# Seven products instead of eight: the second half's output projection of a hybrid decoder layer by Strassen's scheme

## The chip, the cores and the metric

The kernel runs on one NeuronCore of one Trainium2 chip. Its time is the device time in microseconds (us) of one execution; shown is the median of several. The engines are TensorE (PE, with its weight loads as PEld), VectorE (DVE), ScalarE (ACT), GpSimd (POOL) and SyncE (SP), which here issues every DMA. Each engine works through its own instructions in order and waits on semaphores for the others.

## The reference

One layer over 1024 tokens of 1024 channels in float32. A mixer, made of a recurrence over 8 heads (RWKV-7) and a causal convolution of width 31, each giving 512 channels, is followed by an output projection, and that by a gated feed-forward part with a short convolution; each is normed before and after and added to its input. What the change touches is one line:

```python
x = x + _rms_norm(mix, norm_post_mix)       # mix = concatenate([rwkv_out, c]) @ w_out
#   rwkv_out: 1024 tokens x 512      c: 1024 tokens x 512      w_out: 1024 x 1024
h = _rms_norm(x, norm_pre_ffn)              # and from here the feed-forward part
```

For one half of the tokens (512) this product is 512 x 1024 by 1024 x 1024. Cut into two by two blocks, the activations are A11 (first 256 tokens, recurrent channels), A12 (first 256 tokens, convolution channels), A21 and A22 (the last 256 tokens); the weight has blocks B11 to B22 of 512 x 512.

## The kernel before, in words

The tokens are handled in two halves of 512 and, in the mixer, in quarters of 256; a quarter has four chunks of 64, which the recurrence takes one after the other. Every matrix product is done with operands split into a rounded high part and a low remainder (`split`: ACT casts the high part, then POOL or DVE subtracts it from the source), and three matmuls per pair of tiles: high x high, high x low, low x high. A weight tile of 256 KB is brought by `weight`: an SP DMA into one of the raw buffers (tag `wr`, three in pool `wp`, and two more in pool `wq` that only the feed-forward part uses), an ACT cast, and a subtraction by POOL, or by DVE where `low_pool` is false.

`mixer` writes the work as streams with priorities (`PRIO`); a scheduler puts each engine's instructions in an order worked out from priorities and from estimated times. The recurrence and what prepares it come first (`rwkv`), then the norm of the first half for the feed-forward part (`top`), norms, convolution, and last projections (`proj`), which fill TensorE where the others wait. `prepare(q)` runs the four recurrence chunks of quarter q-1 between the steps that prepare quarter q; `finish` norms and gates a quarter's result into `mixr`, a tile of 512 channels x 512 tokens. `conv` and `conv_norm` give the four `co` tiles. While the last quarter's recurrence runs (`prepare(4)`), the first nine blocks of the first half's feed-forward part (`EARLY`, `ffn_pair`, 48 matmuls each) fill TensorE.

Then `w_out(1, ...)` projects the second half. All eight activation tiles are split into four `l8` buffers, the split waiting for `W[3].merged`. For each of four groups of 256 output columns and each of eight row tiles of the weight, two tiles of rows to a load, there are four token tiles and three matmuls of 256 columns. `evac` multiplies a finished bank by the post-norm's weight (`post_mix`), squares it on ACT with a sum per token into `ssq`, and stores the product to `mixd` in DRAM. The load of the second column group's first weight is the mark `self.start`: loads of the feed-forward stage are issued behind it, so that the first gate matmuls (`gates`) can run between the groups. `norm_ffn(1, ...)` reads `ssq` and `mixd` back.

The feed-forward part already has a product of this kind: `ffn_down` by seven products, with its weight sums made on POOL by `four_sums` in `weight_sums`.

Of the kernel before, what the change touches and what calls it, by code (L numbers as in the profile page):

```python
# [22 lines left out]
P = 128  # L23
# [3 lines left out]
HALF = 512  # L27
QUARTER = 256
# [8 lines left out]
CONV_W = 31  # L37
# [10 lines left out]


BUFS = {"v": 2, "gd": 1, "pt": 6, "kk": 1, "l8": 5, "ca": 6, "ck": 6, "r": 2,  # L50
        "mixr": 1, "co": 4, "po": 1, "c": 4, "t2": 2}

EARLY = 9

JOINT = 13
PLAIN = FT - JOINT

RAW, MORE_RAW, PAIRS, MORE_PAIRS = 3, 2, 2, 1

PRIO = {"first": -1000, "top": 100000, "rwkv": 1000, "norm": 200000, "conv": 300000, "proj": 400000}  # L60


PARAMS = [
# [37 lines left out]
class Trunk:  # L101
# [62 lines left out]
    def split(self, hi, lo, src, pool=False):  # L164

        eng = self.nc.gpsimd if pool else self.nc.vector
        return self.nc.scalar.copy(hi, src), eng.tensor_tensor(lo, src, hi.bitcast(F32), ALU.subtract)  # L167

    def wtile(self, tag, shape, dt=F32):

        pool = next(self.homes[tag]) or self.wp
        bufs = {self.wp: (RAW, PAIRS), self.wq: (MORE_RAW, MORE_PAIRS)}[pool][tag != "wr"]
# [28 lines left out]
    def setup(self):  # L201
        nc, tc, ctx, a = self.nc, self.tc, self.ctx, self.a
        pool = lambda name, **kw: ctx.enter_context(tc.tile_pool(name=name, bufs=1, **kw))
        self.cp = pool("const")
        self.small = ctx.enter_context(tc.tile_pool(name="small", bufs=4))
        self.wp = ctx.enter_context(tc.tile_pool(name="wp", bufs=1))
        self.wq = ctx.enter_context(tc.tile_pool(name="wq", bufs=1))
        self.hp = ctx.enter_context(tc.tile_pool(name="hp", bufs=2 * KT))
        self.dp = pool("dram", space=DRAM)
        self.rowp = pool("rowp")  # L210
        self.psum = pool("psum", space=PSUM)
        cp = self.cp
# [12 lines left out]
        self.lows = self.dp.tile([22, 2, P, 4, P], F32, name="lows")  # L225
        self.sums = self.dp.tile([4, HT, P, 512], F32, name="sums")
        self.plain = self.dp.tile([PLAIN, P, HALF], F32, name="plain")
        self.usums = self.dp.tile([4, P, 512], F32, name="usums")
        self.ecarry = cp.tile([P, 2, 12, 2], F32, name="ecarry")

# [65 lines left out]
    def pair(self, what, pool):  # L296
        return tuple(pool.tile([P, HALF], F32R, tag="h", name=self.nm(what)) for _ in range(2))
# [534 lines left out]
        return mark  # L832


    def setup_ffn(self, ctx):
# [23 lines left out]
    def norm_ffn(self, h, row, piece, hs, ahead=2, tags=("pn",), dg=None, pool=None):  # L859


        nc = self.nc
        rows, diags = [], []
        cut = lambda c: slice(c * 512, (c + 1) * 512)

        def channels(tp):
            if not tp:
                hs.extend(self.pairs("f", pool))
            ts = slice(2 * tp, 2 * tp + 2)
            self.channels(rows[ts], "pre_ffn", hs, slice(tp * 256, (tp + 1) * 256), tags, diags[ts] or None)  # L870
# [3 lines left out]
        nc.vector.tensor_reduce(r[:, 0:4], self.ssq[:, 4 * h:4 * h + 4], AX.X, ALU.add)  # L874
        self.rstd(r[:, 4:8], r[:, 0:4], 1.0 / D, RMS_EPS)
        for t in range(4):
            if t == ahead:
                channels(0)
            tt = 4 * h + t
            rs = slice(tt * P, (tt + 1) * P)  # L880
            x, s = row(), sf[:, t]
            nc.sync.dma_start(x, self.a["x"][rs])
            for c in range(2):
                m = piece()
                nc.sync.dma_start(m, self.mixd[rs, cut(c)])
                nc.vector.scalar_tensor_tensor(x[:, cut(c)], m, r[:, 4 + t:5 + t], x[:, cut(c)], ALU.mult, ALU.add)
                nc.scalar.activation(m, x[:, cut(c)], AF.Square, accum_out=s[:, c:c + 1])
            nc.sync.dma_start(self.x1d[rs], x)
            nc.vector.tensor_tensor(s[:, 2:3], s[:, 0:1], s[:, 1:2], ALU.add)
            self.rstd(s[:, 3:4], s[:, 2:3], 1.0 / D, RMS_EPS)  # L890
            if dg is None:
                nc.scalar.activation(x, x, AF.Copy, scale=s[:, 3:4])
            else:
                nc.vector.tensor_scalar(dg[:, t], self.con("ident"), s[:, 3:4], None, ALU.mult)
                diags.append(dg[:, t])
            rows.append((x[:, :512], x[:, 512:]))
            yield
        if ahead == 4:
            channels(0)
            yield  # L900
        channels(1)
# [363 lines left out]
    def mixer(self, sts):  # L1265
        nc, tc = self.nc, self.tc
        W = [None] * 4
        mixes = [None] * 2

        def project(h, hs, names):  # L1270
            with self.stream("proj"):
                for n in names.split():
                    if n == "w":
                        self.wa_in(h, hs, sts[h])
                    elif n == "g":
                        self.gate_in(h, hs, sts[h])
# [74 lines left out]
        with self.stream("norm"):  # L1351
            two = [self.tl("l8", [P, 2, D]) for _ in range(2)]
# [3 lines left out]
            hs = self.pairs("h")  # L1356
# [21 lines left out]
        hs = self.pairs("h")  # L1378
# [25 lines left out]
        conv_norm(1)  # L1404
        with self.stream("proj"):
            piece = lambda: self.tl("pt", [P, HALF])
            for i in range(EARLY):
                if i % 2 == 0:
                    two = self.row("row", 4)
                nc.sync.dma_start(self.early[i], self.ffn_pair(0, h0, i, piece, two[:, i % 2 * HALF:(i % 2 + 1) * HALF]))  # L1410
# [77 lines left out]
```

## Time and profile before

| | |
|---|---|
| three runs | 1251.70, 1251.86, 1258.57 us |
| median | 1251.86 us |
| profiled execution | 1257.58 us, span 1255.8 us |
| granted TensorE clock in it | 0.985 |
| TensorE busy | 1210.4 us (96%) |
| DVE, ACT, POOL busy | 72%, 58%, 40% |
| second half's output projection | 640.34 to about 698.3 us of the span |

A row of the windows view is one stretch: its ends and length, then for PE, PEld, DVE, ACT and POOL the busy time with the number of instructions, then the granted clock, the share of the DMA engines, and GB/s. A row of the timeline is start, duration, engine, line, operation, written tile <- read tiles, and in brackets the idle time before it with what ended it. The chain of waits gives start, duration and the instruction group on the path that ended last. A row of a tile or line view gives the shortest, median and longest duration, the first and last start. L140 is the matmul helper, L155 the transpose helper, L167 `split`, L184 the weight's DMA.

### The profile page before, as it was taken

What the parts mean: (1) busy time and instruction counts of PE and PEld (TensorE: products, weight loads), DVE (VectorE), ACT (ScalarE), POOL (GpSimd) and SP (SyncE); (2) the same over time, 40 slices, a digit from 0 to 9 for tenths busy, and PEclk for the clock granted to TensorE, in tenths of its full rate; (3) what the DMA queues carried; (4) which work ended last, traced back from release to release, by engine and by line L of the source; (5) the groups of instructions that cost most, each with busy time, mean ns of one, the idle gap of its engine ahead of it and who ended that gap; (6) DMA issues with size and microseconds to landing.
All of it is one profiled execution on the core that took longest, in us unless ns stands there. A gap on an engine that the chain in (4) does not pass through costs nothing.

```text
span 1255.8 us, 22979 instructions
## 1 busy us (share of the span) xinstructions
PE 1210.4 (96%) x8424; PEld 988.9 (79%) x8424; DVE 899.8 (72%) x1558; ACT 729.1 (58%) x1515; POOL 507.1 (40%) x447
## 2 busy tenths in 40 slices
PE   5999999999999998999999999999999999999997
PEld 4767777787778876778889888888888888888885
DVE  5285998898669989998640555666656679479667
ACT  7563564565955676466762576876555566554451
POOL 4343330001103331344563399998888850000002
PEclk9999998999999989999999999999999999999999
DMA  7644442333343353222364798894322335336413
GB/s 243 177 131 137 129 135 64 97 128 119 114 128 91 97 178 110 75 80 85 104 186 118 271 323 293 298 315 153 82 74 81 101 134 166 95 117 219 134 52 134
DMA packets 102912, 180.97 MB, mean 144 GB/s; under 512 B 14896, under 2 KB 21424, under 8 KB 102800
## 3 DMA queue, kind: packets, MB, share of 16 engines
q1 hardware_dynamic: 102800, 179.51, 45.6%
q8 instruction: 66, 1.08, 0.4%
q14 instruction: 46, 0.38, 0.1%
HBM read 138.44 MB, written 41.03 MB: 143 GB/s over the span
## 4 chain that ended last, share of the span: by engine, by line
PE 62%; DVE 6%; ACT 2%; issue 1%; DMA 1%; POOL 1%; POOLq 0%; DVEq 0%; ACTq 0%
PE pb L140 27%; PE xs L140 16%; PE pe L140 14%; PE Y L140 2%; PE pc L140 2%; DVE pc L431 2%; DMA pt<-mixd 1%; PE pc L155 1%; PE pe L155 0%; DVE x L1120 0%; DVE m L167 0%; DVE sub L606 0%; DVE nrow L1136 0%; DVE dw L608 0%; DVE t L797 0%
## 5 line engine op out<-in xcount | busy, mean ns | idle before, releaser
L167 POOL TENSOR_TENSOR wl<-wr,wh 128x512 fp32r<-128x512 f32 (+1 forms) x175 | 230.0, 1316 | 219.4 <-ACT wh L167 191.3
L140 PE MATMUL pb<-h,wh 128*128 128x512 f32 (+3 forms) x720 | 230.1, 399 | 2.5 <-ACT wh L167 1.0
L167 ACT CAST wh<-wr 128x512 fp32r<-128x512 f32 (+1 forms) x214 | 131.4, 615 | 131.8 <-issue 42.3
L140 PE MATMUL pb<-f,wh 128*128 128x512 f32 x648 | 205.0, 397 | 2.7 <-ACT wh L167 1.7
L431 DVE SCALAR_TENSOR_TENSOR pc<-c,params,pc 128x512 f32<-128x512 f32 x232 | 174.2, 751 | 8.7 <-ACT pc L428 4.7
L140 PEld LDWEIGHTS pb<-h,wh 128*128 128x128 f32 (+2 forms) x720 | 132.1, 189 | 35.4 <-ACT wh L167 2.7
L140 PE MATMUL pb<-h,wl 128*128 128x512 f32 (+3 forms) x360 | 146.8, 408 | 2.3 <-POOL wl L167 2.1
L140 PEld LDWEIGHTS pb<-f,wh 128*128 128x128 f32 x648 | 121.8, 190 | 28.8 <-ACT wh L167 2.1
L140 PE MATMUL pb<-f,wl 128*128 128x512 f32 x324 | 129.2, 399 | 0.9 <-POOL wl L167 0.9
L162 POOL TENSOR_TENSOR ss<-var,mhalf 128x1 f32<-128x1 f32 x16 | 11.4, 716 | 223.8 <-DVE var L161 223.0
L1076 POOL TENSOR_TENSOR b<-b,b 128x512 f32<-128x512 f32 x72 | 93.3, 1298 | 1.9 <-DMA wr<-ffn_up 0.5
L140 PEld LDWEIGHTS pb<-h,wl 128*128 128x128 f32 (+2 forms) x360 | 67.8, 188 | 20.5 <-POOL wl L167 4.0
L140 PE MATMUL xs<-f,wh 128*128 128x512 f32 x240 | 74.2, 390 | 0.4 <-DVE act L973 0.4
L167 POOL TENSOR_TENSOR wl<-b,wh 128x512 fp32r<-128x512 f32 x48 | 66.6, 1388 | 16.9 <-ACT wh L167 14.9
L140 PEld LDWEIGHTS pb<-f,wl 128*128 128x128 f32 x324 | 61.7, 190 | 14.8 <-POOL wl L167 1.7
L167 ACT CAST wh<-b 128x512 fp32r<-128x512 f32 x48 | 29.7, 618 | 60.0 <-PE pb L140 20.5
L140 PE MATMUL pe<-f,wh 128*128 128x512 f32 x208 | 64.1, 389 | 0.0
L721 POOL TENSOR_TENSOR XG<-r,GE 64x256 f32<-64x256 f32 x30 | 20.5, 683 | 89.3 <-DVE r L740 84.5
L140 PEld LDWEIGHTS xs<-f,wh 128*128 128x128 f32 x240 | 44.9, 188 | 10.0 <-DVE act L973 0.8
L192 ACT CAST wh<-wr 128x512 fp32r<-128x512 f32 (+2 forms) x44 | 26.5, 604 | 44.4 <-PE pb L140 31.2
L167 ACT CAST a<-act 128x512 fp32r<-128x512 f32 x50 | 30.0, 620 | 33.6 <-PE Y L140 19.1
L167 ACT CAST w<-wr 128x512 fp32r<-128x512 f32 x38 | 23.4, 622 | 40.7 <-PE Y L140 20.0
(419 smaller groups left out, 2952.3 us busy)
## 6 DMA issues: line engine op xcount, KB each, us to landing
wr<-ffn_up SPq DMA_DIRECT2D x99, 256.0 KB, 3.2
wr<-w_in SPq DMA_DIRECT2D x80, 256.0 KB, 2.9
b<-ffn_up SPq DMA_DIRECT2D x52, 256.0 KB, 2.7
b<-ffn_down SPq DMA_DIRECT2D x44, 256.0 KB, 4.5
sums<-b SPq DMA_DIRECT2D x44, 256.0 KB, 4.2
wr<-sums SPq DMA_DIRECT2D x44, 256.0 KB, 2.8
lows<-wl SPq DMA_DIRECT2D x40, 256.0 KB, 3.3
wl<-lows SPq DMA_DIRECT2D x40, 256.0 KB, 2.7
```

The lines of the kernel that those rows point to most:

```text
L140: return self.nc.tensor.matmul(out, lhsT, rhs, start=start, stop=stop, skip_group_check=skip)
L155: self.nc.tensor.transpose(out, in_, self.con("ident")[:n, :n])
L162: self.nc.gpsimd.tensor_tensor(out, v[:, :n], self.mhalf[:, :n], ALU.pow)
L167: return self.nc.scalar.copy(hi, src), eng.tensor_tensor(lo, src, hi.bitcast(F32), ALU.subtract)
L192: self.nc.scalar.copy(hi, raw)
L431: nc.vector.scalar_tensor_tensor(out, c[:, j:j + HALF], w(j), acc, ALU.mult, ALU.add)
L721: nc.gpsimd.tensor_tensor(x[64:128], R[64:128, gs], w.GE[64:128, c, gs].unsqueeze(2).broadcast_to([64, 4, CH]), ALU.mult)
L1076: sub = lambda o, x, y, op=ALU.subtract: self.nc.gpsimd.tensor_tensor(o, x, y, op)
```

## The change

The second half's projection becomes seven products of 256 x 512 by 512 x 512 (`w_out_shared`). Each has four row tiles of the weight, two token tiles and three matmuls of 512 columns. The sums of weight blocks (four for each row tile) are made by POOL with `four_sums` while the mixer runs, in a stream of the lowest priority behind project(1)'s `u0`, and stored in DRAM (`wsums`). The sums of activations are made by DVE in place or in freed `v` buffers, and the sums of products by DVE from PSUM. The first product, A11 x B11, is written ahead of the last early feed-forward block, its result copied to SBUF by ACT. In products 3 to 7 the low parts of the weights come by turns from DVE and POOL. The mark for the feed-forward loads is the 21st weight load. Pool `wq` is opened in the feed-forward stage only, which makes room for four `ws` buffers in the mixer.

```diff
-        "mixr": 1, "co": 4, "po": 1, "c": 4, "t2": 2}
+        "mixr": 1, "co": 4, "po": 1, "c": 4, "t2": 2, "ws": 4}
+START = 20
+LAST = 1
-PRIO = {..., "proj": 400000}
+PRIO = {..., "proj": 400000, "sums": 500000}
...
-        self.wq = ctx.enter_context(tc.tile_pool(name="wq", bufs=1))     # in setup
+        self.wq = pool("wq")                                             # in setup_ffn
+        self.wsums = self.dp.tile([4, 4, P, 512], F32, name="wsums")
...
+    def w_out_tile(self, k, c):
+        return self.a["w_out"][2 * c:2 * c + 2, k // 2, :, k % 2].rearrange("e p n -> p e n")
+    def w_out_sums(self):
+        for k in range(4):
+            b = [self.tl("ws", [P, 512]) for _ in range(4)]
+            for n in range(4):
+                nc.sync.dma_start(two(b[n]), self.w_out_tile(4 * (n // 2) + k, n % 2))
+            self.four_sums(*b, b[3])
+            for n, t in ((3, 3), (1, 1), (2, 0), (4, 2)):
+                nc.sync.dma_start(self.wsums[n - 1, k], b[t])
+    def w_out_shared(self, mixr, co, between):
...
+        A11 = split(a11)
...
+        def product(banks, src, acts, start, stop, turn=(False, True)):
+            hi, lo = acts
+            for k in range(4):
+                self.low_pool = turn[k % 2]
+                wh, wl = self.weight(src(k), [P, 2, 256], (self.mix, "ca", "ck"))
+                self.low_pool = True
+                self.marks.append(self.load)
...
+                for t in range(2):
+                    ts = slice(t * P, (t + 1) * P)
+                    self.mm(banks[t], hi[:, k, ts], wh, start=start and k == 0, stop=False, skip=True)
+                    self.mm(banks[t], hi[:, k, ts], wl, start=False, stop=False, skip=True)
+                    self.mm(banks[t], lo[:, k, ts], wh, start=False, stop=stop and k == 3, skip=True)
+        def out(src, q, c):
+            with self.tc.high_priority():
+                for t in range(2):
+                    o = self.tl("c", [P, CONV_W - 1 + HALF])[:, :512]
...
+                    nc.vector.tensor_tensor(o, src[t], post[c], ALU.mult)
+                    nc.scalar.activation(src[t], src[t], AF.Square, accum_out=self.ssq[:, tile_, c:c + 1])
+                    nc.sync.dma_start(self.mixd[tile_ * P:(tile_ + 1) * P, c * 512:(c + 1) * 512], o)
...
+        product(first, B(0, 0), A11, True, True, (True, True))
...
+                nc.scalar.copy(u[t], first[t])
+        between()
+        A12 = split(a12)
+        s3 = spare()
+        tt(s3, a11, a21, ALU.subtract)
+        each(a21, lambda k: a21[:, k], lambda k: a22[k], ALU.add)
+        s2 = spare()
+        tt(s2, a21, a11, ALU.subtract)
+        S2 = split(s2)
+        S1 = split(a21)
+        y = [self.bank("pe") for _ in range(2)]
+        product(y, B(1, 0), A12, True, True, (True, True))
+        add(y, u, y)
+        out(y, 0, 0)
+        x = self.xs
+        product(x, T(2), S2, True, True)
+        S3 = split(s3)
+        add(u, u, x)
+        y = [self.bank("pe") for _ in range(2)]
+        product(y, T(1), S1, True, True)
+        w = [self.tl("ws", [P, 512]) for _ in range(2)]
+        each(s2, lambda k: a12[k], lambda k: s2[:, k], ALU.subtract)
+        S4 = split(s2)
+        add(w, u, y)
+        z = [self.bank() for _ in range(2)]
+        product(z, T(3), S3, True, True)
+        A22 = split(a22)
+        add(x, w, z)
+        out(x, 1, 1)
+        product(y, B(1, 1), S4, False, True)
+        add(y, u, y)
+        out(y, 0, 1)
+        product(z, T(4), A22, False, True)
+        add(z, u, z)
+        out(z, 1, 0)
+        return self.marks[START]
...
-        project(1, hs, "u0 u1 u2 u3")
+        project(1, hs, "u0")
+        with self.stream("sums"), tc.issue_after(self.load.ins):
+            self.w_out_sums()
+        project(1, hs, "u1 u2 u3")
...
-            for i in range(EARLY):
+            for i in range(EARLY - LAST):
+                block(i)
         prepare(4)
         with self.stream("proj"):
-            self.start = self.w_out(1, mixes[1], [sts[1]["co", i] for i in range(4)], W[3].merged)
+            self.start = self.w_out_shared(mixes[1], [sts[1]["co", i] for i in range(4)],
+                                           lambda: [block(i) for i in range(EARLY - LAST, EARLY)])
```

More of the change, by code (lines that the diff above doesn't have):

```diff
@@ L56 @@
 PLAIN = FT - JOINT
+START = 20
+LAST = 1
 RAW, MORE_RAW, PAIRS, MORE_PAIRS = 3, 2, 2, 1
-PRIO = {"first": -1000, "top": 100000, "rwkv": 1000, "norm": 200000, "conv": 300000, "proj": 400000}
+PRIO = {"first": -1000, "top": 100000, "rwkv": 1000, "norm": 200000, "conv": 300000, "proj": 400000, "sums": 500000}
 PARAMS = [
@@ L171, in wtile @@
         pool = next(self.homes[tag]) or self.wp
-        bufs = {self.wp: (RAW, PAIRS), self.wq: (MORE_RAW, MORE_PAIRS)}[pool][tag != "wr"]
+        bufs = ((RAW, PAIRS) if pool is self.wp else (MORE_RAW, MORE_PAIRS))[tag != "wr"]
         return pool.tile(shape, dt, tag=tag, bufs=bufs, name=self.nm(tag))
@@ L832, in w_out @@
         return mark
+    def w_out_tile(self, k, c):
+        return self.a["w_out"][2 * c:2 * c + 2, k // 2, :, k % 2].rearrange("e p n -> p e n")
+    def w_out_sums(self):
+        nc = self.nc
+        two = lambda t: t.rearrange("p (e n) -> p e n", e=2)
+        for k in range(4):
[5 more added lines that the diff above has]
+                nc.sync.dma_start(self.wsums[n - 1, k], b[t])
@@ new lines, in w_out_shared, with pair, split, spare @@
+    def w_out_shared(self, mixr, co, between):
+        nc = self.nc
+        early, later = slice(0, QUARTER), slice(QUARTER, HALF)
+        f = lambda t: t.bitcast(F32)
+        tt = nc.vector.tensor_tensor
+        def pair():
+            t = self.tl("l8", [P, 2, 4, QUARTER], F32R)
+            return t[:, 0], t[:, 1]
+        def split(src):
+            hi, lo = pair()
+            if isinstance(src, list):
+                for k in range(4):
+                    self.split(hi[:, k], lo[:, k], src[k])
+            else:
+                self.split(hi, lo, src)
+            return hi, lo
+        def spare():
+            return self.tl("v", [P, 2, HALF]).rearrange("p l (b t) -> p (l b) t", b=2)
+        def each(out, x, y, op):
+            for k in range(4):
+                tt(out[:, k], x(k), y(k), op)
+        a11, a21 = mixr[:, :, early], mixr[:, :, later]
+        a12, a22 = ([t[:, ts] for t in co] for ts in (early, later))
+        A11 = split(a11)
+        post = [self.tl("c", [P, CONV_W - 1 + HALF])[:, :512] for _ in range(2)]
+        for c in range(2):
+            nc.sync.dma_start(post[c], self.a["post_mix"][:, c * 512:(c + 1) * 512].broadcast_to([P, 512]))
+        def product(banks, src, acts, start, stop, turn=(False, True)):
+            hi, lo = acts
+            for k in range(4):
+                self.low_pool = turn[k % 2]
+                wh, wl = self.weight(src(k), [P, 2, 256], (self.mix, "ca", "ck"))
+                self.low_pool = True
+                self.marks.append(self.load)
+                wh, wl = (w.rearrange("p e n -> p (e n)") for w in (wh, wl))
+                for t in range(2):
[7 more added lines that the diff above has]
+                    o = self.tl("c", [P, CONV_W - 1 + HALF])[:, :512]
+                    tile_ = 4 + 2 * q + t
+                    nc.vector.tensor_tensor(o, src[t], post[c], ALU.mult)
+                    nc.scalar.activation(src[t], src[t], AF.Square, accum_out=self.ssq[:, tile_, c:c + 1])
+                    nc.sync.dma_start(self.mixd[tile_ * P:(tile_ + 1) * P, c * 512:(c + 1) * 512], o)
+        def add(outs, xs, ys):
+            with self.tc.high_priority():
+                for o, x, y in zip(outs, xs, ys):
+                    tt(o, x, y, ALU.add)
+        B = lambda r, c: lambda k: self.w_out_tile(4 * r + k, c)
+        T = lambda n: lambda k: self.wsums[n - 1, k].rearrange("p (e n) -> p e n", e=2)
+        self.marks = []
+        first = [self.bank() for _ in range(2)]
+        product(first, B(0, 0), A11, True, True, (True, True))
+        u = [self.tl("ws", [P, 512]) for _ in range(2)]
+        with self.tc.high_priority():
+            for t in range(2):
+                nc.scalar.copy(u[t], first[t])
[34 more added lines that the diff above has]
+        return self.marks[START]
@@ L873, in norm_ffn @@
         sf = self.small.tile([P, 4, 4], F32, tag="sf", bufs=1, name=self.nm("sf"))
-        nc.vector.tensor_reduce(r[:, 0:4], self.ssq[:, 4 * h:4 * h + 4], AX.X, ALU.add)
+        nc.vector.tensor_reduce(r[:, 0:4], self.ssq[:, 4 * h:4 * h + 4, :2 if h else 4], AX.X, ALU.add)
         self.rstd(r[:, 4:8], r[:, 0:4], 1.0 / D, RMS_EPS)
@@ L1406, in mixer, with block @@
             piece = lambda: self.tl("pt", [P, HALF])
-            for i in range(EARLY):
+            def block(i):
                 if i % 2 == 0:
-                    two = self.row("row", 4)
-                nc.sync.dma_start(self.early[i], self.ffn_pair(0, h0, i, piece, two[:, i % 2 * HALF:(i % 2 + 1) * HALF]))
+                    two[:] = [self.row("row", 4)]
+                nc.sync.dma_start(self.early[i], self.ffn_pair(0, h0, i, piece, two[0][:, i % 2 * HALF:(i % 2 + 1) * HALF]))
+            two = []
+            for i in range(EARLY - LAST):
+                block(i)
         prepare(4)
         with self.stream("proj"):
-            self.start = self.w_out(1, mixes[1], [sts[1]["co", i] for i in range(4)], W[3].merged)
+            self.start = self.w_out_shared(mixes[1], [sts[1]["co", i] for i in range(4)],
+                                           lambda: [block(i) for i in range(EARLY - LAST, EARLY)])
         return h0
```

## The prediction

> **What bounds the kernel now.** I read the page first, then the busy time by stretches, then TensorE's own order of time around the second half's output projection.
>
> ```profile
> span 1255.8 us, 22979 instructions
> PE 1210.4 (96%) x8424; PEld 988.9 (79%) x8424; DVE 899.8 (72%) x1558; ACT 729.1 (58%) x1515; POOL 507.1 (40%) x447
> 320.00:360.00 40.00, 37.59 (x288) 29.33 (x287) 26.16 (x55) 31.19 (x69) 5.82 (x7) 1.00 0.35 106
> 360.00:400.00 40.00, 37.57 (x215) 30.30 (x214) 35.68 (x71) 21.10 (x40) 6.12 (x7) 0.96 0.32 100
> 520.00:600.00 80.00, 79.91 (x737) 63.82 (x729) 72.13 (x110) 48.00 (x105) 35.59 (x30) 1.00 0.29 85
> 624.00:640.00 16.00, 13.38 (x53) 10.03 (x52) 13.04 (x17) 13.64 (x27) 8.77 (x6) 0.91 0.36 114
> 640.00:698.00 58.00, 57.64 (x435) 55.42 (x434) 7.62 (x11) 19.27 (x51) 25.99 (x20) 1.00 0.51 146
> 700.00:900.00 200.00, 199.62 (x897) 164.99 (x896) 124.13 (x194) 140.04 (x296) 172.85 (x139) 1.00 0.78 263
> ```
>
> The columns after the stretch and its length are PE, PEld, DVE, ACT and POOL busy, granted clock, DMA share, GB/s. TensorE is the bound: 79.91 of 80 us, 57.64 of 58, 199.62 of 200. Holes are in the mixer (2.4 us in each of 320 to 360 and 360 to 400) and between 624 and 640 (2.6 us, at clock 0.91). So the change is worth what it takes off TensorE's work, plus holes closed, less holes opened. TensorE's timeline of the place:
>
> ```profile
> 632.64 0.39 PE L140 MATMUL pb<-f,wl 128*128 128x512 f32 x1
> 634.74 0.73 PE L140 MATMUL pb<-f,wh 128*128 128x512 f32 x2 [1.70 <-ACT wh L167]
> 636.39 0.50 PE L140 MATMUL pb<-f,wl 128*128 128x512 f32 x1 [0.92 <-POOL wl L167]
> ...
> 639.91 0.62 PE L140 MATMUL pb<-f,wl 128*128 128x512 f32 x1
> 640.34 11.71 PE L140 MATMUL pb<-wm,l 128*128 128x256 f32 x96
> ```
>
> Up to 639.91 this is the ninth early feed-forward block; at 640.34 the output projection begins. From 633.03 (end of the first row) to 640.34 only 12 matmuls run: x2 and x1 at the two waits, and three more such threes. The chain of waits then gives the paces:
>
> ```profile
> 652.05 11.52 PE xs L140 x96
> 666.33 5.47 PE xs L140 x24
> 683.31 5.47 PE pe L140 x24
> 688.78 8.76 PE pb L140 x73
> 698.28 2.13 DMA mixd<-t
> ```
>
> A matmul of 256 columns takes 11.52/96 = 0.120 us of the chain, one of 512 columns 5.47/24 = 0.228 us. The two groups of 24 are feed-forward gate blocks that already fill in behind the projection.
>
> **The change part by part. Matmuls.** Removed: 4 column groups x 8 row tiles x 4 token tiles x 3 (high and low parts) = 384 matmuls of 256 columns, 384 x 0.120 = 46.1 us. Check: 640.34 to 698.28 is 57.9, less 2 x 5.47 of filler 47.0. Added: 7 products x 4 x 2 x 3 = 168 matmuls of 512 columns, 168 x 0.228 = 38.3 us. TensorE saves **7.8 us**, all of it on the path, since TensorE is full. [...]
>
> **The hole at 633.** ACT's timeline shows what TensorE waited for:
>
> ```profile
> 628.78 1.28 ACT L452 ACT_TABLE_LOAD   x1
> 630.08 1.51 ACT L452 ACTIVATE co<-pc,params 128x128 f32<-128x128 f32 x4
> 631.46 0.63 ACT L167 CAST wm<-wr 128x512 fp32r<-128x512 f32 x1
> 631.97 2.19 ACT L167 CAST l<-co 128x512 fp32r<-128x512 f32 x4
> 634.05 0.63 ACT L167 CAST wh<-wr 128x512 fp32r<-128x512 f32 x1
> ```
>
> The ninth block's cast stood behind the convolution's last norm and the activation casts, which only the projection needs. The 7.31 us held 12 x 0.228 = 2.7 us of work, so the hole with its slow clock cost 4.6 us. After the change the first product (5.5 us; it needs only the early-token quarter of `mixr`) stands ahead of this block, and A12, S2 and S1 are needed only after the block. The last `co` lands at 631.6; the sum S1 (four of 0.42 us), S2 (1.25) and its split (ACT about 1.2, DVE 1.25) end near 637. The ninth block begins near 640.34 - 4.6 - 48 x 0.228 = 624.8 now; with the first product ahead of it, both are done at 624.8 + 5.5 + 10.9 = 641.2, and S2 is asked for only a product later, at 646.7. That is 9 us of cover, so I take the hole as closed: **4.6 us**. If the casts again queue ahead of the block's, nothing of it is won. (The 0.42 and 1.25 are these rows; they are 256 and 1024 elements wide.)
>
> ```profile
> L774 DVE TENSOR_TENSOR mixr<-mixr,pt 128x256 f32<-128x256 f32 x16 | 6.6, 420 | 5.7 <-ACT mixr L770 5.7
> L564 DVE TENSOR_TENSOR l<-l,gd 128x1024 f32<-128x1024 f32 x8 | 10.0, 1255 | 9.9 <-PE pe L140 9.9
> ```
>
> **Feeding the products.** Before, a weight load of 256 KB served 24 matmuls of 256 columns, 2.9 us; now it serves 6 of 512, 1.37 us. The raw buffers stay three.
>
> ```profile
> wr<-w_out SPq DMA_DIRECT2D x32, 256.0 KB, 2.8
> L167 ACT CAST wm<-wr 128x512 fp32r<-128x512 f32 x16 | 9.9, 621 | 11.5 <-PE xs L140 5.7 <-PE pb L140 3.6 <-DMA wr<-w_out 1.5
> L167 POOL TENSOR_TENSOR wm<-wr,wm 128x512 fp32r<-128x512 f32 x13 | 16.8, 1291 | 9.4 <-ACT wm L167 9.3
> L167 DVE TENSOR_TENSOR wl<-wr,wh 128x512 fp32r<-128x512 f32 x39 | 26.7, 685 | 0.6 <-ACT wh L167 0.6
> ```
>
> A buffer's turn is 2.8 (landing) + 0.62 (cast) + 0.99 (mean of POOL's 1.29 and DVE's 0.69, which alternate in products 3 to 7) = 4.4 us; over three buffers 1.47 us a weight against 1.37. Behind the first product stand 24 weights: 35.3 us of feeding against 32.8 of matmuls. The lower bound is 0 (six pair buffers, filled under the ninth block). The upper: DVE and POOL hold each other up. The same split of `co` took DVE 1118 ns a piece beside POOL and 680 without:
>
> ```profile
> L167 DVE TENSOR_TENSOR l<-co,l 128x512 fp32r<-128x512 f32 x4 | 4.2, 1118 | 1.1 <-ACT l L167 1.1
> L167 DVE TENSOR_TENSOR m<-co,m 128x512 fp32r<-128x512 f32 x4 | 2.6, 680 | 0.0
> 598.65 1.28 POOL L167 TENSOR_TENSOR wl<-wr,wh 128x512 fp32r<-128x512 f32 x1 [0.86 <-ACT wh L167]
> 598.74 1.74 DVE L932 TENSOR_TENSOR row<-pt,pt 128x512 f32<-128x512 f32 x1
> 567.86 0.68 DVE L932 TENSOR_TENSOR row<-pt,pt 128x512 f32<-128x512 f32 x1
> ```
>
> The DVE multiplication L932 took 1.74 instead of 0.68 us, to just after POOL's end at 599.93 plus its own time. In products 3 to 7 POOL's ten lows (12.9), DVE's ten lows (6.9), the splits of S3 and S4, the four differences and A22's four lows (about 6) make 25.8 us that must not overlap, in 27.3 us of matmuls. With a further 1 us of such waiting in each buffer's turn a weight takes 1.8 us: 43.2, that is 10.4 us lost. I take **2.5 us**, nearer the rows without waiting, as DVE is busy only 7.6 of 58 us there now. [...]
>
> **Sums of the product's vectors.** 14 additions from PSUM and 8 multiplications of 0.69 us on DVE, 8 squares and 2 copies on ACT (about 0.6): the only ones that could hold TensorE are those that free a bank, and each bank is asked for again a product (5.5 us) later, against some 3.5 us of work. Cost 0; if DVE's queue is late, this is part of the 10.4 above. After the last product gate matmuls follow in other banks, as now at 698. They are let in from the 21st load on, so holes of products 2 to 5 stay unfilled.
>
> **Weight sums in the mixer.** 16 POOL operations, 16 loads, 16 stores.
>
> ```profile
> L1076 POOL TENSOR_TENSOR b<-b,b x72: 1279/1295/1352, 724.5 to 1010.5; 128x512 f32<-128x512 f32 x72
> 383.32 1.27 POOL L167 TENSOR_TENSOR wl<-wr,wh 128x512 fp32r<-128x512 f32 x1 [3.14 <-DMA wr<-w_out]
> 382.04 0.18 DVE L608 TENSOR_TENSOR dw<-dw,sub 128x26 f32<-128x26 f32 x1
> 383.58 1.06 DVE L606 TENSOR_TENSOR sub<-dw 128x36 f32<-128x36 f32 x1
> L193 SPq DMA_DIRECT2D wl<-lows x23: 319/320/524, 283.8 to 377.3; - x23
> ```
>
> The last row places them: 23 of the second half's 44 loads of stored low parts (k, w, r, then u0 as the 19th to 22nd) come from 283.8 on, so the sums stand from about 284 to 340.
>
> 16 x 1.295 = 20.7 us of POOL, which has 5.8 of 40 us busy in 320 to 360, so POOL has room. But each can hold DVE as at 383.58: 1.06 instead of about 0.18, 0.88 us. Sixteen such are 14.1 us of DVE time; none is the lower end. DVE is idle 13.8 of 40 us there, and TensorE has the early blocks as cover from 520 on, so I take **1 us**. On SP's queue the stores wait for POOL, and project(1)'s loads stand behind them: at worst 4 sets x (5.2 us of sums, less 2.7 us for the weight ahead) = 10 us, at best nothing. I take 0, because in 700 to 900 the same pattern of stores runs with TensorE at 199.62 of 200. Moving the second weight pool (`wq`) into the feed-forward stage costs 0: its place was the mixer's constants, which are read for the last time ahead of the output projection, and the gate loads come after its 21st load.
>
> **Sum.** 7.8 + 4.6 - 2.5 - 1 = 8.9 us. The profiled execution took 1257.6 us (span 1255.8); it becomes 1248.7. The runs shown are 1251.70, 1251.86 and 1258.57, so the profiled one is like the longest. Applied to the median 1251.86: **1243 us**. One per cent, 12.5 us, is about what a measurement of this kernel can tell from no change.
>
> **The rivals.** *Everything flows.* Nothing lost in feeding or in the mixer: 12.4 us, 1239.4, a little less if a mixer hole closes too. For it: DVE nearly idle at 640 to 698. Against: 1.47 us a weight. Chance 0.18.
>
> *Feeding becomes the bound.* The upper price of 10.4 replaces 2.5: 8.9 - 7.9 = 1.0 us, 1251. For it: 25.8 of 27.3 us on DVE and POOL together, one in-order DVE queue that also carries the bank sums, and no filler before the 21st load. Against: six pair buffers ahead. Chance 0.20.
>
> *The sums in the mixer hold DVE.* Place: 284 to 340, where POOL would run 16 operations beside the chain of the recurrence. Price: 14.1 us, of which each that reaches TensorE opens a hole. It decides from 9.9 us on (12.4 less 2.5); at 14.1 the kernel is slower by 4.2: 1256. Against: TensorE has projections to do there. Chance 0.12.
>
> *The hole stays* (the scheduler's order leaves the casts ahead, so the moved block does nothing): 8.9 - 4.6 = 4.3 us, 1247.6. Inside the range; I count it with the forecast, whose band of 1239.5 to 1249 has 0.50.
>
> **How the numbers follow.** Range 1235 to 1257: from some 4 us under the full gain (mixer holes) to just over the slower rival. Faster by over 1% (under 1239.3): half of "everything flows" and the forecast's lower edge, with the execution-to-execution spread of 7 us, 0.21. Slower by over 1% (over 1264.4): the slower rival together with bound feeding, 0.07. Within 1%: 0.72.
>
> **What would show it.** Matmuls of `wm` 168 of 512 columns, 38 us together; no wait of over 1 us on L167 between the eighth early block and the second product; in products 2 to 7 TensorE's waits on ACT, POOL or DVE lows together near 2.5 us; the POOL sums somewhere from 284 to 340, and TensorE's busy time from 280 to 520 within 1 us of now. A granted clock under 1.0 during the products, or DVE operations of two SBUF inputs at 1.1 us and more all along them, would mean the feeding rival. The prediction is wrong if the reordering by the scheduler moves other mixer work by more than these terms.

## The result, and the profile after

The changed kernel takes **1273.35 us** (median of 6 runs, 1270.94 to 1276.24) against 1253.79 (1251.7 to 1258.57) for the kernel before beside it: ratio 1.0155, 95% interval 1.0133 to 1.0177. It is 1.55% slower. 1243 was forecast, in a range of 1235 to 1257, with 0.07 for slower by over 1%.

The page after, span and busy time (the profiled execution took 1276.24 us):

```profile
span 1274.5 us, 22686 instructions
PE 1210.9 (95%) x8208; PEld 980.4 (77%) x8208; DVE 931.5 (73%) x1595; ACT 737.5 (58%) x1518; POOL 530.0 (42%) x465
```

TensorE has 216 matmuls fewer and is busy just as long as before (1210.4). A busy time is not work: here it grew where the clock was low (14 `pe` matmuls took 1.16 us at 473.62, at clock 1.00 from 473.6 to 474.8, and 2.04 us at 482.43, at 0.50 from 482.4 to 484.5; the granted clock is 0.57 from 480 to 500). The span is 18.7 us longer. Where that arises is read best from a fixed mark. The store of the first early feed-forward block (tile `early`, first and last start) stands behind most of the mixer's work (the last quarter's recurrence still runs) and ahead of everything that the products touch. Before, then after (the code has more lines now: L1541 was L1410, `split` is L171, the matmul helper L144, the transpose helper L159, the weight's load L188, the load of stored low parts L197):

```profile
L1410 SPq DMA_DIRECT2D early<-row x9: 326/327/327, 521.7 to 644.0; - x9
```

```profile
L1541 SPq DMA_DIRECT2D early<-row x9: 320/327/441, 536.3 to 681.2; - x9
```

**14.6 us are lost before that mark**, and from it to the end of the span 738.2 us pass instead of 734.1, **4.1 more where 9.9 less were forecast**. (The two traces are of long executions: 3.8 us over the median before, 2.9 after.) The loss ahead of the mark shows at two places. The windows of before, then of after:

```profile
280.00:340.00 60.00, 59.04 (x454) 46.20 (x451) 48.98 (x88) 40.99 (x87) 11.82 (x16) 1.00 0.41 124
280.00:520.00 240.00, 226.84 (x2387) 186.96 (x2386) 204.86 (x398) 150.18 (x328) 59.03 (x64) 0.97 0.38 116
460.00:480.00 20.00, 18.17 (x230) 13.07 (x228) 13.96 (x34) 10.29 (x31) 4.78 (x6) 0.84 0.64 209
480.00:500.00 20.00, 16.91 (x175) 13.22 (x173) 19.28 (x50) 16.52 (x40) 3.61 (x6) 1.00 0.20 70
```

```profile
280.00:340.00 60.00, 55.94 (x393) 43.38 (x392) 48.07 (x80) 38.12 (x78) 33.03 (x32) 1.00 0.73 238
280.00:520.00 240.00, 220.19 (x2061) 181.73 (x2060) 194.59 (x378) 141.83 (x313) 75.28 (x75) 0.94 0.46 143
460.00:480.00 20.00, 13.01 (x163) 9.16 (x162) 13.63 (x28) 12.34 (x34) 4.52 (x6) 0.83 0.66 206
480.00:500.00 20.00, 18.67 (x152) 15.81 (x152) 11.36 (x31) 7.03 (x19) 2.70 (x5) 0.57 0.32 115
```

From 280 to 340, where the sums run, TensorE loses 3.1 us of work and the DMA share rises from 0.41 to 0.73. From 460 to 480, long after the last sum, it loses 5.2 us, and from 480 to 500 it runs at clock 0.57. Its timeline there:

```profile
477.29 0.41 PE L159 MATMUL xs<-const,v 128*64 128x128 f32 x2 [1.33 <-DVE r L744]
480.61 0.70 PE L144 MATMUL pe<-l,l 64*128 64x128 f32 x2 [2.92 <-DVE ca L560]
482.43 2.04 PE L144 MATMUL pe<-l,l 64*128 64x128 f32 x14 [0.72 <-DVE ca L560]
```

The `pe` bank that is asked for at 477.7 has yet to be read by DVE (`ca`, L560, in `scores` of the last quarter), which first does steps of a norm and of `finish` and comes to it at 479.71. Behind that matmul in TensorE's queue stands the recurrence chunk of the quarter before (L744 is the chunk's own step), so the chunk waits too, and no projection's matmul stands in the timeline from 473 to 500 to fill in.

In the products, the chain of waits leaves TensorE. It runs through two loads of `w_out` (2.80 us at 651.61 and 2.73 at 656.44), then through DVE:

```profile
663.79 1.96 DVE l L171 x2
665.74 0.60 issue
666.34 0.77 DVE v L880 x3
667.76 2.23 DVE l L171
669.99 0.60 DVE wm L171
670.59 0.66 DVE pt L1047
671.25 0.60 DVE pe L915
...
678.75 0.60 DVE wm L171
...
698.50 5.44 PE xs L144 x24
```

Splits of activation sums (`l`), a sum (`v`), the low part of a weight (`wm`), a tap of the moved ninth block (L1047), an addition of products (L915): one queue, one after another. GpSimd's holds are among them: the split of 1024 columns at 667.68 took 2.31 us beside a low part on GpSimd, the one at 665.20 took 1.21 without. From 660 to 680 DVE is busy 19.22 of 20 us and TensorE 13.89, at clock 0.88. The last row gives the pace of a 512-column matmul where nothing is late, 5.44/24 = 0.227 us.

### The profile page after: what moved, and what is told of

The parts are those of the page before. It is cut to its first block, busy times and chain, and to the rows that moved or that the text cites. A ratio compares the mean times of both kernels' runs of the same rounds, so it can differ in the third digit from the quotient of the medians.

```text
span 1274.5 us, 22686 instructions
## 1 busy us (share of the span) xinstructions
PE 1210.9 (95%) x8208; PEld 980.4 (77%) x8208; DVE 931.5 (73%) x1595; ACT 737.5 (58%) x1518; POOL 530.0 (42%) x465
## 4 chain that ended last, share of the span: by engine, by line
PE 73%; DVE 14%; ACT 5%; issue 3%; DMA 2%; POOL 2%; SPq 0%; POOLq 0%; DVEq 0%; ACTq 0%
PE pb L144 36%; PE xs L144 17%; PE pe L144 16%; DVE pc L435 4%; PE Y L144 2%; PE pc L144 2%; POOL wl L171 1%; PE pe L159 1%; DVE l L171 1%; DVE pt L504 1%; PE pc L159 1%; DVE dw L612 1%; DVE h L298 1%; DVE pt L1047 1%; DMA pt<-mixd 1%
## 5 line engine op out<-in xcount | busy, mean ns | idle before, releaser
L171 POOL TENSOR_TENSOR wl<-wr,wh 128x512 fp32r<-128x512 f32 (+1 forms) x175 | 229.5, 1313 | 212.0 <-ACT wh L171 186.8
L144 PE MATMUL pb<-h,wh 128*128 128x512 f32 (+3 forms) x720 | 229.6, 398 | 1.6 <-ACT wh L171 1.0
L144 PE MATMUL pb<-f,wh 128*128 128x512 f32 x648 | 203.0, 394 | 4.6 <-ACT pb L909 2.1
L171 ACT CAST wh<-wr 128x512 fp32r<-128x512 f32 (+1 forms) x214 | 131.4, 615 | 126.3 <-PE pb L144 48.4
L435 DVE SCALAR_TENSOR_TENSOR pc<-c,params,pc 128x512 f32<-128x512 f32 x232 | 174.2, 751 | 10.4 <-ACT pc L432 6.2
L144 PEld LDWEIGHTS pb<-h,wh 128*128 128x128 f32 (+2 forms) x720 | 131.4, 188 | 33.1 <-ACT wh L171 2.6
L144 PE MATMUL pb<-h,wl 128*128 128x512 f32 (+3 forms) x360 | 145.9, 405 | 5.8 <-DMA wl<-lows 3.7
L144 PEld LDWEIGHTS pb<-f,wh 128*128 128x128 f32 x648 | 120.9, 188 | 29.6 <-ACT pb L909 2.5
L144 PE MATMUL pb<-f,wl 128*128 128x512 f32 x324 | 128.9, 398 | 0.0
L144 PEld LDWEIGHTS pb<-h,wl 128*128 128x128 f32 (+2 forms) x360 | 67.7, 188 | 24.5 <-DMA wl<-lows 4.8
L144 PE MATMUL xs<-f,wh 128*128 128x512 f32 x240 | 74.1, 391 | 0.2 <-DVE act L1101 0.2
L171 POOL TENSOR_TENSOR wl<-b,wh 128x512 fp32r<-128x512 f32 x48 | 66.0, 1376 | 18.6 <-ACT wh L171 16.9
L144 PEld LDWEIGHTS pb<-f,wl 128*128 128x128 f32 x324 | 61.1, 189 | 13.0 <-POOL wl L171 0.2
L144 PE MATMUL pe<-f,wh 128*128 128x512 f32 x208 | 64.6, 390 | 0.0
L171 ACT CAST wh<-b 128x512 fp32r<-128x512 f32 x48 | 29.7, 618 | 59.6 <-PE pb L144 20.9
L144 PEld LDWEIGHTS xs<-f,wh 128*128 128x128 f32 x240 | 44.9, 188 | 9.8 <-DVE act L1101 0.6
L171 ACT CAST a<-act 128x512 fp32r<-128x512 f32 x50 | 30.0, 620 | 33.4 <-PE Y L144 18.9
L171 ACT CAST w<-wr 128x512 fp32r<-128x512 f32 x38 | 23.4, 622 | 41.5 <-PE Y L144 20.0
```

The costliest lines, as they stand in the source:

```text
L144: return self.nc.tensor.matmul(out, lhsT, rhs, start=start, stop=stop, skip_group_check=skip)
L435: nc.vector.scalar_tensor_tensor(out, c[:, j:j + HALF], w(j), acc, ALU.mult, ALU.add)
```

## The experiments

Three theories. **A**: the sums' own work (GpSimd beside DVE, 32 transfers) costs the time in the mixer. **B**: not their work but the order: the planner, given 48 more instructions, arranges everything else differently. **C**: the products starve. "First store" is the first early store, read from each trace. There is one trace for each kernel, and kernels with the same mixer order and no sums have it at 518.7 to 521.9, so shifts of up to about 3 us say nothing.

| run | median us | ratio to before, 95% interval | first store |
|---|---|---|---|
| after | 1273.35 | 1.0155 [1.0133, 1.0177] | 536.3 |
| e1 no sums | 1260.89 | 1.0057 [1.0035, 1.0079] | 520.6 |
| e2 sums, old order | 1267.62 | 1.0107 [1.0085, 1.0130] | 526.4 |
| e3 after's order, no sums | 1267.64 | 1.0110 [1.0091, 1.0130] | 526.5 |
| e4 sums early | 1270.70 | 1.0136 [1.0116, 1.0156] | 529.8 |
| e5 = e1, nine blocks ahead | 1257.59 | 1.0026 [1.0016, 1.0036] | 518.7 |
| e6 = e1, no activation sums | 1258.96 | 1.0035 [1.0022, 1.0049] | 519.0 |
| e7 = e2, transfers alone | 1266.04 | 1.0086 [1.0061, 1.0111] | 525.5 |
| e8 = e2, additions alone | 1264.67 | 1.0076 [1.0060, 1.0092] | 524.3 |
| e9 = e5, no activation sums | 1259.21 | 1.0039 [1.0026, 1.0051] | 521.0 |
| e10 = e5, five raw buffers | 1254.62 | 1.0006 [0.9992, 1.0020] | 521.9 |
| e11 = e5, lows on GpSimd | 1259.39 | 1.0043 [1.0028, 1.0058] | 519.0 |
| e12 = e2, GpSimd's queue | 1269.78 | 1.0120 [1.0100, 1.0141] | 526.8 |
| e13 = e2, spread transfers | 1263.85 | 1.0087 [1.0071, 1.0103] | 523.4 |
| e14 all repairs | 1255.24 | 1.0011 [1.0000, 1.0022] | 522.2 |
| e15 = e14, S3 second | 1264.31 | 1.0083 [1.0068, 1.0099] | 525.3 |

### Work, order and products taken apart: e1, e2, e3

e1 leaves the sums out. Products 3 to 5 and 7 read plain blocks of the weight, here and in e3, e5, e6 and e9 to e11, so what these compute is not the layer:

```diff
-        project(1, hs, "u0")
-        with self.stream("sums"), tc.issue_after(self.load.ins):
-            self.w_out_sums()
-        project(1, hs, "u1 u2 u3")
+        project(1, hs, "u0 u1 u2 u3")
-        T = lambda n: lambda k: self.wsums[n - 1, k].rearrange("p (e n) -> p e n", e=2)
+        T = lambda n: lambda k: self.w_out_tile(4 * (n // 3) + k, n % 2)
```

e2 and e3 build the kernel twice, once with the sums and once without, and queue every engine's other instructions in the order of the other build. The added dependencies fix the order of issue only; nobody waits for a result.

```diff
+def follow(tc, made, order):      # order: each engine's instructions as the other build has them
...
+        for a, b in zip(seq, seq[1:]):
+            tc.add_manual_dep(b, a.name, mybir.DependencyInfo(
+                mybir.DependencyClass.NoSync, mybir.DependencyReason.DATA), reason="order")
```

> After without the weight sums: no loads, additions or stores in the mixer, and products 3 to 5 and 7 read plain blocks of w_out in place of the stored sums (so its output is not the layer's; the products keep their number, shapes and splits). In the mixer every engine's order is then that of before. Theory A (the sums' own work in the mixer, on GpSimd's port and in the DMA queues, costs about 14 us) and theory B (not their work: the planner, given the sums, put the mixer's other instructions in another order, and that order costs about 14 us) both expect the early blocks back at the times of before (first store near 522) and 1250 to 1258. Theory C (the products lose by themselves what they save: their feeding costs over 15 us) expects 1265 or more.

> After with the sums where they are, but every other instruction of each engine is queued in the order that the planner makes without the sums (that of run e1). Theory A: the sums' work is all there, so as slow as after, 1268 to 1275, first early store near 536. Theory B: as fast as e1 within 4 us, first early store 521 to 525.

> After's order on every engine, but without the sums (as in e1, products 3 to 5 and 7 read plain blocks of w_out). Theory A: the loss goes with the sums, 1250 to 1260, first early store 521 to 526. Theory B: the loss stays with the order, 1266 to 1275, first early store 532 to 537.

The first store of e1, e2 and e3:

```profile
L1538 SPq DMA_DIRECT2D early<-row x9: 326/327/339, 520.6 to 665.1; - x9
```

```profile
L1546 SPq DMA_DIRECT2D early<-row x9: 319/327/338, 526.4 to 670.7; - x9
```

```profile
L1546 SPq DMA_DIRECT2D early<-row x9: 320/327/575, 526.5 to 671.0; - x9
```

No theory has it all: e1 lies between the ranges of A and B and that of C, e2's time and first store lie between A's and B's, and e3 has B's time but a first store 5.5 us ahead of B's. Against 1253.64 beside them, the products alone cost 7.2 us (e1), the sums' work 6.7 more (e2 less e1), the order alone 6.7 more (e3 less e1). Together, before rounding, 20.7, where the whole change costs 19.6: the three nearly add up.

Where the order's loss arises, e3 shows with no sum anywhere. DVE's order in it is e1's up to 312 us. Paired by name with e1's, its DVE instructions are in the median 3.1 us ahead from 400 to 440 and 4.0 us behind from 480 to 500. The window from 460 of e1, then of e3:

```profile
460.00:480.00 20.00, 17.23 (x234) 12.65 (x230) 15.05 (x37) 11.26 (x34) 4.79 (x7) 0.91 0.66 217
```

```profile
460.00:480.00 20.00, 13.57 (x129) 9.70 (x130) 12.16 (x29) 9.30 (x26) 4.49 (x7) 0.76 0.63 216
```

and e3's TensorE timeline has the same wait as after's, 5.0 us earlier:

```profile
475.58 0.76 PE L144 MATMUL pe<-l,l 64*128 64x128 f32 x2 [2.92 <-DVE ca L560]
```

By the first store the 5.0 us between the two have become 9.8. The stretch at half clock lies between: from 480 to 500 e3 has clock 0.96, the kernel after 0.57. So order and sums together cost more here than each alone; why the clock stays low in one of them only is open.

The sums' loss is not all beside the sums either. The wait for `mixr` (L779) that e1 has at 388.60 e2 has at 391.30, 2.7 us later; at the first store it is 5.8. In between, two low parts on GpSimd that took 1.92 and 1.47 us in e1 took 6.13 us in e2, with the same instructions around them, only later:

```profile
397.93 6.13 POOL L171 TENSOR_TENSOR wl<-wr,wh 128x512 fp32r<-128x512 f32 x2 [7.36 <-ACT wh L171]
402.87 0.39 PE L144 MATMUL pb<-wl,m 128*128 128x256 f32 x1 [2.15 <-POOL wl L171]
```

### What the sums' work costs: e4, e7, e8, e12, e13

> After with the same sums placed in the first half, behind project(0)'s u2 and u3, where TensorE and DVE have the planner's order of e1. Theory A: the sums hold DVE and the DMA queues there too, so slower than e1 by 5 to 15 us, 1260 to 1270. Theory B: within 3 us of e1. If e1 is below the kernel before by what the products save, this version is faster than before as well: 1243 to 1250.

> Run e2 (old order, sums in place; it was 6.7 us above e1) without GpSimd's 16 additions: the 16 loads and 16 stores stay, the stored tiles are plain blocks. If the cost is that of the transfers (DMA queues, SP's queue), 1265 to 1269 and the first early store near 526; if it is GpSimd's hold on DVE, 1259 to 1263 and near 521.

> Run e2 with one set of four loads and four stores in place of four sets; GpSimd does all 16 additions, on the same four buffers (products 3 to 5 and 7 read the one stored set). If the cost is GpSimd's hold on DVE, 1264 to 1269 and the first early store near 526; if it is that of the transfers, 1260 to 1263 and near 522.

> Run e2 (old order, sums in place, 6.7 us above e1) with the 16 loads and 16 stores of the sums issued by GpSimd in place of SyncE. If the loss is that project(1)'s stored low parts stand behind the sums' transfers in SyncE's queue, most of it goes: 1261 to 1264, first early store near 522, no wait of TensorE for lows over 1 us at 284 to 330. If it is the load on the DMA engines, or GpSimd's hold on DVE and on the recurrence's own GpSimd operations, it stays: 1266 to 1272.

> Run e2 (old order; sums cost 6 us up to the first early store) with the sums' 32 transfers spread singly over the 44 weight loads of the second half's projections, each store two weights behind its addition; GpSimd's 16 additions stay. If bunched transfers in SyncE's queue and in the DMA engines are the loss, the first early store comes at 520 to 523 and the time is 1260 to 1263; if GpSimd's hold on DVE and on the recurrence is enough, near 524 to 526 and 1264 to 1268.

The edits to `w_out_sums`, one per run (e4 moves its call behind `project(0, hs, "u2 u3")`):

```diff
-            self.four_sums(*b, b[3])                                   # e7
+            if k == 0:                                                 # e8: loads of one set alone
+        for n, t in ((3, 3), (1, 1), (2, 0), (4, 2)):                  # e8: and its stores, behind all 16 additions
+            nc.sync.dma_start(self.wsums[n - 1, 0], b[t])
-                nc.sync.dma_start(two(b[n]), self.w_out_tile(4 * (n // 2) + k, n % 2))   # e12, stores likewise
+                nc.gpsimd.dma_start(two(b[n]), self.w_out_tile(4 * (n // 2) + k, n % 2))
+                yield                                                  # e13: behind each transfer
+        if kept and kept[0] and self.steps is not None:                # e13: in weight(), a step for each load
+            self.step_sums()
```

e4 shows the mechanism at one place. SyncE's queue, then TensorE:

```profile
206.55 3.04 SPq L853 DMA_DIRECT2D wsums<-ws  x3
209.63 1.24 SPq L850 DMA_DIRECT2D ws<-w_out  x2
210.92 1.37 SPq L853 DMA_DIRECT2D wsums<-ws  x1
212.39 0.37 SPq L197 DMA_DIRECT2D wl<-lows  x1
```

```profile
216.03 0.79 PE L144 MATMUL pb<-h,wl 128*128 128x512 f32 x1 [3.91 <-DMA wl<-lows]
```

The low part that lets TensorE go on at 216.03 was issued at 212.39. From 206.55 to there SyncE's queue had held transfers of the sums alone: stores that wait for GpSimd's additions, and loads of the next set that wait for the stores. The kernel after has the same waits, smaller, in its TensorE and SyncE waits from 270 to 340:

```profile
PE pb L144 <- DMA wl<-lows: 3.7, 3, 1.4
```

```profile
SPq L853 <- POOL ws L1204: 12.4, 11, 1.9
SPq L853 <- DMA ws<-w_out: 9.4, 4, 3.9
```

e4 is 9.8 us above e1, within theory A's 5 to 15 (1270.7 is just over its 1270) and far from B's 3. Up to the mark DVE and ACT have e1's order in it, so the sums' work costs more in the first half. e7 meets what was expected if the transfers are the cost, and e8, at 1264.67, what was expected if GpSimd is. So they do not separate the two: the additions alone (with a quarter of the transfers) move the first store by 3.7 us, the transfers alone by 4.9, both together by 5.8. e12 moves the transfers out of SyncE's queue, and the waits for `lows` vanish. Others take their place:

```profile
PE pc L160 <- DVE t L454: 3.5, 2, 1.8
PE pc L160 <- ACT co L459: 2.0, 2, 1.4
PE pe L160 <- DVE mixr L768: 1.6, 2, 1.4
```

`t` and `mixr` need the small powers (`rstd`) that GpSimd makes for the norms, now queued behind GpSimd's own transfers and the additions that wait for them: in e12 the input of one is ready at 314.25, and it runs at 318.25, behind three additions and two stores. GpSimd spent 0.74 us on issuing each load and 0.59 on each store. So 6 us stay, as the second expectation said; whether by this queue or by the load on the DMA engines, e12 does not separate. Another issuer alone gave nothing back here: the first store is 6.2 us behind e1's, in e2 5.8. e13 shows what helps: one transfer per weight load, each store two weights behind its addition. The first store comes at 523.4, no wait for `lows` is left from 280 to 360, and 3.8 of the 6.7 us are back, a little less than was expected of bunched transfers (1260 to 1263). Spreading thins both SyncE's queue (one transfer between two weight loads) and the load on the DMA engines (their busy share is 0.81 from 280 to 300 and 0.78 from 300 to 320 in e2, 0.55 from 280 to 320 in e13), so this does not tell the two apart either.

### What the products cost: e5, e6, e9, e10, e11

> Run e1 (no weight sums) with all nine early blocks ahead of the first product, none moved behind it. Theory M (the moved ninth block is what takes the product stage's cover: its convolution step stands in DVE's and ACT's queues ahead of the last convolution tiles and of the activation sums, which came 9 us later in e1): activation sums end earlier, TensorE's waits from product 3 on fall by 5 us or more, 1250 to 1256. Theory F (three raw buffers and the splits between DVE and GpSimd set the pace of the products wherever they begin): 1259 to 1264.

> Run e1 with the sums of activations left out as well: products 3 to 6 take splits of A11, A21 and A11, A21 in place of S2, S1, S3, S4 (seven splits and all weights stay), so DVE loses two subtractions of 1024 columns and eight of 256 and product 3 waits for no convolution tile. Theory S (the chain of activation sums on DVE behind the last convolution tile is the loss between product 2 and product 4, about 9 us): 1249 to 1254. Theory F (feeding of the weights): 1258 to 1262.

> Run e5 (no weight sums, nine early blocks ahead; 3.3 us above before) with the sums of activations left out as in e6. If DVE's serial chain of activation sums and their splits is what starves products 3 and 4 (TensorE waited 4.5 us for one low part of DVE in e5), 1250 to 1254; if the three raw buffers set the pace, 1256 to 1258.

> Run e5 in e5's order on every engine, but with five raw weight buffers during the products in place of three (two products' sums lie in other buffers for it). If the raw buffers' turn sets the pace of the products (ACT waits of 2.6 to 2.9 us for a weight's landing in e5), 1251 to 1255; if DVE and GpSimd do, within 1 us of e5, 1257 to 1258.5.

> Run e5 with every low part of the products' weights on GpSimd, none on DVE. If the wait for a low part that stands behind activation sums in DVE's queue is the loss, 1253 to 1256; if GpSimd's 1.3 us for each weight against 1.37 us of matmuls, with its hold on DVE, costs as much, 1257 to 1262.

```diff
-LAST = 1                                                               # e5, e9, e10, e11
+LAST = 0
-        tt(s3, a11, a21, ALU.subtract)                                 # e6, e9: and the other three sums
+        S2 = split(a11)
+        self.homes["wr"] = cycle([self.wp] * RAW + [self.wx] * 2)      # e10, in w_out_shared
-        def product(banks, src, acts, start, stop, turn=(False, True)):
+        def product(banks, src, acts, start, stop, turn=(True, True)): # e11
```

e1's ACT and DVE at the moved block:

```profile
638.09 0.62 ACT L171 CAST wm<-wr 128x512 fp32r<-128x512 f32 x1 [3.71 <-DMA wr<-w_out]
...
639.85 1.51 ACT L456 ACTIVATE co<-pc,params 128x128 f32<-128x128 f32 x4
```

```profile
639.99 0.75 DVE L1047 SCALAR_TENSOR_TENSOR pt<-pb,params,pt 128x511 f32<-128x511 f32 x1 [8.52 <-ACT ecarry L1040]
```

The last convolution tile came at 630.08 before; here it comes at 639.85, behind a cast that waits 3.7 us for a load of w_out and behind the ninth block's own steps. DVE stands idle for 8.5 us ahead of the ninth block's tap, with the activation sums queued behind it. Ahead again (e5), the block gives 3.3 us back; 1257.59 lies between the two expected ranges. But the last `co` comes no earlier:

```profile
638.47 1.50 ACT L456 ACTIVATE co<-pc,params 128x128 f32<-128x128 f32 x4
```

From the first store it is 108.4 us to this point before, 119.3 in e1 and 119.8 in e5. So the moved block is not what makes `co` late. Already the transposes with which its norm begins (`pc` from `co`) come 97.8 us from the first store before, 107.6 in e1 and 107.1 in e5, ahead of the products' matmuls in e5 (631.75). What delays them no run tests. What is left in e5, DVE and then TensorE's waits:

```profile
643.37 2.36 DVE L171 TENSOR_TENSOR l<-v,l 128x1024 fp32r<-128x1024 f32 x1 [1.11 <-ACT l L171]
645.65 1.21 DVE L171 TENSOR_TENSOR l<-mixr,l 128x1024 fp32r<-128x1024 f32 x1
646.79 2.49 DVE L880 TENSOR_TENSOR v<-co,v 128x256 f32<-128x256 f32 x4
649.21 1.21 DVE L171 TENSOR_TENSOR l<-v,l 128x1024 fp32r<-128x1024 f32 x1
650.34 0.68 DVE L171 TENSOR_TENSOR wm<-wr,wm 128x512 fp32r<-128x512 f32 x1
```

```profile
PE xs L144 <- DVE wm L171: 4.5, 1, 4.5
PE pe L144 <- POOL wm L171: 2.8, 3, 1.7
```

The low part of a weight (650.34) stands behind two splits, four subtractions and a third split. e11 moves these lows to GpSimd and loses 1.8 us, as its second expectation said: TensorE now waits for GpSimd's lows (3.5 us from 640 to 700) and for ACT's casts. e6 drops the activation sums and gains 1.9 us, within the range of feeding; e9 drops them and loses 1.6, outside both its ranges. No wait for DVE's lows is left in either, and others take its place: in e9, 4.9 us for banks that ACT's squares (L909) have yet to read and 2.1 for a cast. The last `co` came later still in them (646.18 and 643.18), so they settle little. **e10 helps most**: five raw buffers, the order held, 3.0 us better than e5 (2.3 if each is taken against the runs of before beside it), as expected if the buffers' turn sets the pace, and no measurable difference from before is left (0.9 us). The window over the products of before, then of e10:

```profile
640.00:700.00 60.00, 59.64 (x443) 57.07 (x442) 8.22 (x13) 20.22 (x55) 26.23 (x21) 1.00 0.51 148
640.00:700.00 60.00, 53.78 (x218) 41.32 (x219) 38.85 (x56) 31.39 (x61) 29.49 (x22) 0.97 0.59 186
```

TensorE still lacks 6 us there, and DVE has 38.85 us to do where before had 8.22. The 8 us saved are spent there. That DVE's load is the reason is not shown: in e9 it is 25.67 us, and TensorE's busy time, 52.06, is that of e5 (51.91).

### The repairs together: e14, e15

e14 joins the edits of e5, e10 and e13 and the order without sums. e15 adds:

```diff
+        S3 = split(s3)
+        z = [self.bank() for _ in range(2)]
+        product(z, T(3), S3, True, True, (True, True))
         A12 = split(a12)
...
-        z = [self.bank() for _ in range(2)]
-        product(z, T(3), S3, True, True)
         A22 = split(a22)
```

> All repairs together, the whole layer computed: old order, spread sums as in e13, nine early blocks ahead, five raw buffers in the products (e10 was 0.9 us above before without any sums). If e13's repair holds, 1254 to 1257, the same as before; if the sums still cost 4 us or more, 1258 to 1261.

> Run e14 with the product of A11 - A21, which needs no convolution tile, moved from fifth to second place. If TensorE's wait for the first activation sum behind the late convolution tiles (3.4 us in e10, with a slow clock behind it) is what is left of the products' loss, 3 to 5 us below e14; if GpSimd and DVE only swap which product waits, within 1.5 us of e14.

e14 is 1255.24 us: 18.1 of the 19.6 us are back, as expected, which fits these places. It is also only 0.6 us above e10, which has no sums, though the spread sums cost 3.0 in e13 over e1: the parts do not add up better than that. The layer is no faster than by the plain projection (1.0011, interval 1.0000 to 1.0022). None of the versions run beats the kernel before. e15 is 9.1 us slower than e14; neither expectation holds. Between the two traces (10.9 us) 3.1 lie ahead of the first store, within what says nothing, and 7.8 behind it, so the new order of products costs most of it; through which wait stays open.

## Why the prediction was wrong, step by step

- **Matmuls, 7.8 us saved: right.** 46.1 - 168 x 0.227 = 8.0.
- **The hole at 633, 4.6 us: closed, but moving the block was not needed and cost 3.3.** In e1 no wait for a cast is left there. In e5, where no block is moved, the longest wait of TensorE from 600 to 640 is 0.6 us as well, and e5 is 3.3 us faster than e1.
- **The cover, 9 us from a last `co` at 631.6: gone.** The step took the time of `co` as fixed. With the products it comes some 11 us later from the first store, in e1 and in e5 alike, and the sums of activations with it.
- **Feeding, 2.5 us (bounds 0 and 10.4): the term that failed in the products.** From the first store to the end the traces show 4.1 us more instead of 9.9 less, 14.0 off; by its median e1, which has no sums, lost 7.2. With 7.8 and 4.6 saved, e5's 3.3 us over before mean some 15.7 us of feeding and e10's 0.9 some 13.3: over the upper bound. The buffer's turn was about right: two more buffers gave 3.0. What was missed is that DVE takes weights' lows, activation sums, splits and bank sums in one order, all at once behind the late `co` (18.85 of 20 us busy from 640 to 660 in e5, TensorE 14.51), and that the clock falls behind the longest wait (4.53 us up to 651.07; clock 0.83 in that window; the 22 matmuls behind it took 7.28 us, 5.0 at the pace of 0.227). How much each of these costs is not shown. The feeding rival (1251) named this queue; it priced it without the late start and without the clock, which it gave only as a sign.
- **Sums of the product's vectors, 0: not 0.** Gate matmuls do not all follow in other banks: TensorE waits 2.10 us at 716.46 for a `pb` bank that ACT's squares (L909) have yet to read, and 0.41 earlier for a `pe` bank.
- **Weight sums, 1 us: 6.7 by e2 against e1.** Of the 14.6 us before the first store some 6 are their work. The price for SyncE's queue (0 to 10) was taken at 0 by a stretch, 700 to 900, in which TensorE did not wait for such stores; in the mixer it does, since there a low part is issued shortly before its use (in e4 issued at 212.39 and asked for at 216.03 - 3.91 = 212.12). The hold on DVE, priced at 14.1 for the slower rival, is part of it at most: with a quarter of the transfers 3.7 us remain (e8). That rival had one of the two places right; that its 14.1 is near the 14.6 measured is an accident.
- **Order: not in the sum at all.** 6.7 us by e3 against e1, 5.7 by the kernel after against e2. The text named it as what would make the prediction wrong, and gave it no price and no chance. This is the largest fault of method: a planner that rearranges the mixer for 48 added instructions is a rival, not a footnote.
- Of the signs named, 168 matmuls, no long wait for a split ahead of the second product, and the sums' place (280.8 to 328.3) held. TensorE's busy time from 280 to 520 within 1 us did not: 226.84 became 220.19, and the clock 0.97 became 0.94. Its waits for casts and lows in products 2 to 7 came to 6.9 us instead of 2.5, and the signs of the feeding rival came: clock 0.88 from 660 to 680, and DVE operations held beside GpSimd.

## What to carry to other kernels

Where a planner orders the instructions, an addition has two prices, its work and the new order; build with the old order forced, and each can be measured alone. Transfers that share a queue with just-in-time loads went better here one at a time, with each store two weights behind its addition (3.8 of 6.7 us back in e13). The fewer, larger matmuls turned TensorE's time into preparation on other engines here (from 640 to 700 DVE is busy 8.22 us before and 38.85 in e10): count the busy time per matmul of the engine that feeds them, and ask when the first operand is ready, before counting the saving.

## What was not expected of the hardware

After a gap of 2.92 us (up to 480.61) with small matmuls around it, TensorE in the trace of the kernel after ran at a granted clock of 0.57 from 480 to 500, though 18.67 of those 20 us were busy; before, no 20 us window from 400 to 520 was under 0.84. In e3 the same wait, also 2.92 us, ends at 475.58; its clock is 0.76 from 460 to 480 and 0.96 from 480 to 500. What keeps the clock low for longer in the kernel after, no run here shows.
